# A decoder layer on Trainium2: the split chunks of the output projection moved by 192 bytes in their buffers

## The chip, the cores and the metric

The kernel runs on 1 core of one Trainium2 chip. The metric is device time in microseconds (us) of one launch; lower is better. Before the change the median of 3 runs is 1662.71 us (1659.02 to 1663.55).

## What is computed

One post-norm decoder layer on 256 tokens of width 4096, all in float32:

```python
mod = c @ w_ada[l] + b_ada[l]
shift, scale, gate = jnp.split(mod, 3, axis=-1)
u = x * (1.0 + scale[:, None]) + shift[:, None]
proj = u @ w_in[l]
...
y_rg = _rg_lru(...) * jax.nn.silu(rg_g)
y_nsa = _nsa(...) * jax.nn.silu(nsa_g)
y_hg = _hgrn2(...)
y = jnp.concatenate([y_rg, y_nsa, y_hg], axis=-1) @ w_out[l]
x = _layer_norm(ALPHA * x + (1.0 + gate[:, None]) * y, ln_g[l], ln_b[l])
```

`proj` has 11824 columns that feed three groups of heads: an RG-LRU recurrence (1024 channels), sparse attention (16 heads of 128) and an HGRN2 recurrence (8 heads of 128). `w_out` is 4096 x 4096.

## The kernel before

**Matmuls in three parts.** A float32 product is made of three matmuls in the format float32r: each operand is split into a rounded part and the rest, and hi x hi, hi x lo and lo x hi are accumulated in PSUM. Weights come in chunks of [128, up to 1024] in the order of a list of steps: `load` starts the DMA into a `raw` tile, `split` (line 1037) makes `hi` by a cast on ACT and `lo = raw - hi`, a part of the columns on DVE and the rest on POOL. When PSUM has room, DVE subtracts a second cast that ACT has put into PSUM. Four `hi` and four `lo` buffers go round.

**Order of the work.** `w_ada` is reduced on DVE to shift and scale, block by block of the 4096 input rows (10 blocks); each block's `u` is split into `uh` and `ul`, and the input projection runs over the block's chunks (`mm`, matmul on line 457). There the stationary operand is the 128 x 128 piece of the weight and the moving one is `uh` or `ul` with 256 tokens; for the groups `hg_i`, `vs` and `vw` it is the other way round, and the moving operand is the weight: 256 columns, or 304 for `vw`. In a chunk with three row blocks of `vw` the slices of 304 columns (1216 bytes) follow each other without a gap.

The output projection (`mm` with the matmul on line 969) has 128 chunks of two row blocks and 512 columns. The stationary operand is a 128 x 128 piece of `yh` or `yl`, the split output of a pair of heads; the moving one is the chunk's `hi` or `lo`, 512 columns. A chunk gives 2 token halves x 2 row blocks x 3 = 12 matmuls, so 1536 in all. `PARTS` sets the order: first the pairs 0 to 3 (RG-LRU) and 12 (HGRN2) for all eight column blocks, then 13, 14, 15, 4, 5, then the rest.

**The work between.** The heads' own work is written as fibers, Python generators that yield between pieces; `run_bg` advances them between the matmul groups of the projections when the planner's account of each engine lets it. The instructions are recorded in that order, and each engine executes its own queue in order. Lanes: RG-LRU, HGRN2, attention, and the compressed keys. A fiber of a lane starts when its inputs are done and when its slots fit in the ring (line 1189):

```python
if (all(x in done for x in need)
        and used[0] + cost + sum(max(0, r_[2] - r_[3]) for h_ in heavy for r_ in h_) <= NRING - SPARE):
```

In the HGRN2 fiber the level matmuls stand on line 708 (seven levels, each waiting for products that DVE and POOL make after the one before), the last cross term on 733, the value matmuls on 742 to 744, the sum of squares on 756, the broadcast of the norm on 769. `finish_y` then makes `yh` (ACT) and `yl` (POOL). An output chunk is recorded only once its pair is in `YT`.

**Where tiles lie.** The pool `strm` holds `raw`, `ra`, `aacc`, `hi`, `lo` and `ev`; the pool `ring` begins with a tile `shift` of `SHIFT_W` = 48 words and goes on with 62 slots of 2 KB for everything else of size [128, 512] (`u`, accumulators, the fibers' tiles, `yh`, `yl`). In the built program all `strm` buffers begin at 128 bytes past a multiple of 256, and all ring slots at 64 past one.

A helper records DVE, ACT and POOL instructions, so these show line 119 in the profile.

Of the kernel before, what the change touches and what calls it, by code (L numbers as in the profile page):

```python
# [12 lines left out]
FR = mybir.dt.float32r  # L13
# [5 lines left out]
P = 128  # L19
# [115 lines left out]
def trunk(ctx: ExitStack, tc: tile.TileContext, pack, xT, xz, w_ada, b_row, w_in, w_out, rg_w, w1, w2,  # L135
# [8 lines left out]
    strm = ctx.enter_context(tc.tile_pool(name="strm", bufs=1))  # L144
    ring = ctx.enter_context(tc.tile_pool(name="ring", bufs=1))
    psum = ctx.enter_context(tc.tile_pool(name="psum", bufs=1, space=bass.MemoryType.PSUM))
    NRING, NRAW, NSPL, NRA = 62, 4, 4, 4
    NPS = 5
    cnt = [0]
    live = [0]  # L150
# [1 line left out]
    def nm(s):  # L152
        cnt[0] += 1
        return f"{s}_{cnt[0]}"
# [13 lines left out]
    def ps_x():  # L168
        live[0] += 1
        assert live[0] <= NPS  # L170
        return psum.tile([P, 512], FT, name=nm("ps"), tag="ps", bufs=8)

    def ps_free(n=1):
        live[0] -= n
# [204 lines left out]
    def ada_end(kb, xt=None):  # L379

        n = KB[kb]
        xt = xt or load_x(kb)
        while any(r_[1] == kb for r_ in pending):
            ada_sum()
        acc = []
        for q, ps in enumerate(ada_state.pop(kb)):
            m = min(512, 2 * n * P - 512 * q)
            t_ = strm.tile([P, 512], FT, name=nm("aacc"), tag="aacc", bufs=2)
            act.copy(t_[:, :m], ps[:, :m])
            ps_free()  # L390
            acc += [t_[:, o:o + P] for o in range(0, m, P)]
        yield 1
        pp = ada_state.pop("pe") if kb == 0 else ps_x()
        for q in range(2 * n):
            nc.tensor.matmul(pp[:, q:q + 1], lhsT=acc[q], rhs=ones[:, 0:1],  # L395
                             start=kb > 0, stop=True, skip_group_check=kb == 0)
        yield 0
        md = consts.tile([P, 8], FT, name=nm("md"), tag="md", bufs=2)
        dve.tensor_add(md[:, :2 * n], pp[:, :2 * n], vec("b_mod")[:, 2 * KB0[kb]:2 * KB0[kb] + 2 * n])
        ps_free()  # L400
        dve.tensor_scalar(md[:, :n], md[:, :n], 1.0, None, op0=OP.add)
        yield from make_u(kb, xt, md[:, :n], md[:, n:])
# [25 lines left out]
    for kb in range(NKB):  # L428
        state = {}
        for items, width in chunks(kb):  # L430
            st = Step("win", off, width)
# [516 lines left out]
    for pi, part in enumerate(PARTS):  # L948
        for nb in range(NB):
            state = {}  # L950
            for ci, pr in enumerate(part):
                st = Step("wout", off_o, 1024)
# [84 lines left out]
    def split(st):  # L1037
        if not st.split:
            return
        st.hi = strm.tile([P, st.w], FR, name=nm("hi"), tag="hi", bufs=NSPL)  # L1040
        st.lo = strm.tile([P, st.w], FR, name=nm("lo"), tag="lo", bufs=NSPL)
        m = int(st.w * (1 - POOL_SHARE[st.i >= n_win0])) // 32 * 32
        if m <= 512 and live[0] < HP_PS:
            hp = ps_x()
            act.copy(st.hi, st.raw)
            act.copy(hp[:, :m].bitcast(FR), st.raw[:, :m])
            pool.tensor_sub(st.lo[:, m:], st.raw[:, m:], st.hi[:, m:])
            dve.tensor_sub(st.lo[:, :m], st.raw[:, :m], hp[:, :m])
            ps_free()
            return  # L1050
        act.copy(st.hi, st.raw)
        pool.tensor_sub(st.lo[:, m:], st.raw[:, m:], st.hi[:, m:])
        dve.tensor_sub(st.lo[:, :m], st.raw[:, :m], st.hi[:, :m])
# [5 lines left out]
    def add_at(i, f):  # L1059
        at.setdefault(i, []).append(f)  # L1060
# [8 lines left out]
    for kb in range(1, NKB):  # L1069
# [3 lines left out]
        due += [(a_ + (b_ - a_) * i / n_ch, kb, i) for i in range(n_ch)]  # L1073
        add_at(b - END_AT, lambda kb=kb: fibers.append([ada_end(kb), 1, 0, 0, 0]))
    last_part = NB * sum(map(len, PARTS[:-1]))
# [133 lines left out]
    for i in range(min(AHEAD, N)):  # L1209
        load(order[i])  # L1210
        if i < SA:
            split(order[i])
        for f in at.pop(i - LEAD, []):
            f()
# [3 lines left out]
    for i in range(N):  # L1218
        st, cur[0] = order[i], i
        if i + SA < N:  # L1220
            split(order[i + SA])
# [113 lines left out]
SPARE = 0  # L1335
MARGIN = 5
END_AT = 6


# [63 lines left out]
```

## Time and profile before

| | before |
|---|---|
| median of 3 runs, us | 1662.71 (1659.02 to 1663.55) |
| profiled execution, us | 1660.88 |
| its span, us | 1659.1 |
| mean granted TensorE clock | 0.990 |
| busy: TensorE, DVE, ACT, POOL | 96%, 80%, 59%, 58% |
| HBM read, MB | 485.12 |

The span runs from the first to the last instruction of the profiled execution; its own time is 1.8 us longer. "PE" is TensorE's matmuls, "PEld" its weight loads, which overlap them; "SPq" are DMA issues on SyncE's queue. [...] Starts in the order of time are given to 10 ns.

### The profile page before, as it was taken

To read this page: it belongs to the slowest core of one execution; us is meant where nothing else is said; L and a number is where in the kernel's file an instruction comes from. 1 tells how busy PE (TensorE), PEld (TensorE's weight loads), DVE (VectorE), ACT (ScalarE), POOL (GpSimd) and SP (SyncE) were. 2 spreads that over 40 slices of the span, in tenths; PEclk is the share of its full clock that TensorE was granted. 3 is DMA by queue.
4 is the path that set the end of the run, shared out by engine and by line. 5 is a ranking of instruction groups with operands and counts; after the bars stand their busy time and mean duration, and the time that the engine had idled before them with its cause. 6 is when DMAs were issued, how large, how long until landed. Compare 5 with 4: busy or idle time off the path is not lost.

```text
span 1659.1 us, 33161 instructions
## 1 busy us (share of the span) xinstructions
PE 1597.9 (96%) x11752; PEld 1497.6 (90%) x11752; DVE 1331.8 (80%) x2301; ACT 971.6 (59%) x1557; POOL 954.5 (58%) x765
## 2 busy tenths in 40 slices
PE   4999999999999999999999999889999999999997
PEld 4999999998999999999999998889888888878884
DVE  5668978799788788788787797899689688968875
ACT  2887666665655555555555566763565566656562
POOL 1579987776655455555455446576453445455655
PEclk9999999999999999999999998999999999999998
DMA  7998989999999899899899886767667766689983
GB/s 287 368 344 313 365 292 343 309 370 327 328 351 334 289 347 327 299 351 327 303 333 332 312 300 223 247 230 266 230 230 242 238 204 215 222 296 374 338 318 126
DMA packets 146486, 491.49 MB, mean 296 GB/s; under 512 B 16264, under 2 KB 17288, under 8 KB 146320
## 3 DMA queue, kind: packets, MB, share of 16 engines
q1 hardware_dynamic: 146320, 489.38, 82.5%
q8 instruction: 92, 1.51, 0.4%
q14 instruction: 74, 0.61, 0.1%
HBM read 485.12 MB, written 4.19 MB: 295 GB/s over the span
## 4 chain that ended last, share of the span: by engine, by line
PE 79%; DVE 11%; DMA 3%; issue 3%; ACT 3%; POOL 0%; SPq 0%; DVEq 0%; ACTq 0%
PE mm L457 50%; PE mm L969 21%; DVE ps L119 3%; DVE acc L119 2%; DVE lo L119 2%; DMA ra<-in_w_ada_dram 1%; ACT hi L119 1%; DMA raw<-in_w_in_dram 1%; PE ps L708 1%; DVE rgt L119 1%; PE ps L901 1%; PE ps L1287 1%; DVE rgy L119 1%; PE ps L792 1%; PE ps L395 1%
## 5 line engine op out<-in xcount | busy, mean ns | idle before, releaser
L119 POOL TENSOR_TENSOR lo<-raw,hi 128x576 fp32r<-128x576 f32 (+4 forms) x527 | 707.7, 1344 | 609.3 <-ACT hi L119 588.4
L119 ACT CAST hi<-raw 128x1024 fp32r<-128x1024 f32 (+3 forms) x527 | 529.1, 1004 | 487.3 <-POOL lo L119 220.4
L457 PE MATMUL mm<-uh,hi 128*128 128x256 f32 x2560 | 719.3, 281 | 15.3 <-DVE lo L119 9.2
L457 PE MATMUL mm<-uh,lo 128*128 128x256 f32 x2560 | 714.0, 279 | 1.9 <-DVE lo L119 1.4
L457 PE MATMUL mm<-ul,hi 128*128 128x256 f32 x2560 | 713.6, 279 | 0.0
L119 DVE SCALAR_TENSOR_TENSOR ps<-ra,pk,ps 128x512 f32<-128x512 f32 x744 | 520.8, 728 | 8.7 <-DMA ra<-in_w_ada_dram 2.9
L457 PEld LDWEIGHTS mm<-uh,hi 128*128 128x128 f32 x2560 | 485.3, 190 | 19.0 <-DVE lo L119 11.8
L457 PEld LDWEIGHTS mm<-uh,lo 128*128 128x128 f32 x2560 | 485.1, 189 | 2.6 <-DVE lo L119 1.9
L457 PEld LDWEIGHTS mm<-ul,hi 128*128 128x128 f32 x2560 | 485.6, 190 | 0.3 <-issue 0.2
L119 DVE TENSOR_TENSOR lo<-raw,ps 128x448 fp32r<-128x448 f32 (+4 forms) x500 | 303.2, 607 | 224.3 <-ACT ps L119 182.6
L119 ACT CAST ps<-raw 128x448 fp32r<-128x448 f32 (+4 forms) x500 | 259.5, 519 | 7.2 <-DVE acc L119 6.5
L119 DVE TENSOR_TENSOR acc<-mm,acc 128x512 f32<-128x512 f32 (+1 forms) x346 | 231.5, 670 | 0.0
L969 PE MATMUL mm<-hi,yh 128*128 128x512 f32 x512 | 210.8, 412 | 0.3 <-ACT ev L119 0.3
L969 PE MATMUL mm<-hi,yl 128*128 128x512 f32 x512 | 201.3, 393 | 0.0
L969 PE MATMUL mm<-lo,yh 128*128 128x512 f32 x512 | 200.1, 391 | 0.0
L969 PEld LDWEIGHTS mm<-hi,yh 128*128 128x128 f32 x512 | 96.4, 188 | 23.4 <-issue 5.7
L969 PEld LDWEIGHTS mm<-hi,yl 128*128 128x128 f32 x512 | 96.1, 188 | 21.6
L457 PE MATMUL mm<-hi,uh 128*128 128x256 f32 (+1 forms) x384 | 110.6, 288 | 4.9 <-ACT hi L119 3.0
L969 PEld LDWEIGHTS mm<-lo,yh 128*128 128x128 f32 x512 | 96.5, 188 | 19.1 <-issue 1.2
L457 PE MATMUL mm<-lo,uh 128*128 128x256 f32 (+1 forms) x384 | 108.9, 284 | 0.0
L457 PE MATMUL mm<-hi,ul 128*128 128x256 f32 (+1 forms) x384 | 108.9, 284 | 0.0
L119 POOL TENSOR_TENSOR acc<-ev,acc 128x512 f32<-128x512 f32 x77 | 101.2, 1315 | 2.8 <-ACT ev L119 2.5
(193 smaller groups left out, 1480.0 us busy)
## 6 DMA issues: line engine op xcount, KB each, us to landing
ra<-in_w_ada_dram SPq DMA_DIRECT2D x323, 512.0 KB, 5.8
raw<-in_w_in_dram SPq DMA_DIRECT2D x291, 512.0 KB, 5.1
raw<-in_w_out_dram SPq DMA_DIRECT2D x128, 512.0 KB, 4.6
raw<-in_w_in_dram SPq DMA_DIRECT2D x90, 384.0 KB, 5.2
ra<-in_w_ada_dram SPq DMA_DIRECT2D x64, 384.0 KB, 5.5
ra<-in_w_dram SPq DMA_DIRECT2D x16, 512.0 KB, 3.9
raw<-in_w_ada_dram SPq DMA_DIRECT2D x13, 512.0 KB, 5.6
xz<-in_xz_dram SPq DMA_DIRECT2D x16, 256.0 KB, 6.0
```

The source lines that it names most:

```text
L119: return f(*a, **k)
L395: nc.tensor.matmul(pp[:, q:q + 1], lhsT=acc[q], rhs=ones[:, 0:1], start=kb > 0, stop=True, skip_group_check=kb == 0)
L457: nc.tensor.matmul(dst, lhsT=l_, rhs=r_, start=s and n_ == 0, stop=e and n_ == 2)
L708: nc.tensor.matmul(pl[:, (2 * x + j) * 64:(2 * x + j + 1) * 64], lhsT=k[:, j, x * P:(x + 1) * P], rhs=qp[:, j, x * P:(x + 1) * P].rearrang ...
L792: nc.tensor.matmul(s1[:, b * T:(b + 1) * T], lhsT=q[:, j, P:], rhs=kk[b][:, g], start=True, stop=True)
L901: nc.tensor.matmul(o, lhsT=v0, rhs=eT[:, 0:2], start=b == 0, stop=False)
L969: nc.tensor.matmul(state[x], lhsT=a_, rhs=b_, start=ci == 0 and j == 0 and n_ == 0, stop=ci == len(part) - 1 and j == 1 and n_ == 2)
L1287: nc.tensor.matmul(pb, lhsT=rows[-1 - x], rhs=rows[i // 2][:, i % 2 * 512:i % 2 * 512 + 512], start=True, stop=True)
```

## The change

A chunk of the output projection gets tiles that are 64 words wider and uses them from word 48 on; the chunks of the input projection keep theirs from word 0. The eight buffers grow by 256 bytes each, 2 KB in all, and the ring has one slot less.

```diff
-    NRING, NRAW, NSPL, NRA = 62, 4, 4, 4
+    NRING, NRAW, NSPL, NRA = 61, 4, 4, 4
...
     def split(st):
         if not st.split:
             return
-        st.hi = strm.tile([P, st.w], FR, name=nm("hi"), tag="hi", bufs=NSPL)
-        st.lo = strm.tile([P, st.w], FR, name=nm("lo"), tag="lo", bufs=NSPL)
+
+        o = OUT_AT if st.kind == "wout" else 0
+        st.hi = strm.tile([P, st.w + o * 4 // 3], FR, name=nm("hi"), tag="hi", bufs=NSPL)[:, o:o + st.w]
+        st.lo = strm.tile([P, st.w + o * 4 // 3], FR, name=nm("lo"), tag="lo", bufs=NSPL)[:, o:o + st.w]
...
+OUT_AT = 48
```

In the built program the ring slots are still at 64 past a multiple of 256, the input projection's chunks at 128, the output projection's at 64.

With 61 slots the condition on line 1189 lets some fibers start later, so the recorded order differs from the end of the input projection on. The counts of instructions stay the same for the matmuls and DMAs.

ACT, end of the input projection, before (`hgk` and `acc_677` are tiles of the second HGRN2 fiber, `yh` is an RG-LRU fiber's output, `hi` and `ps` with `raw` are the splits of chunks, `ev` is an evacuation):

```order
L119 CAST ps_15068<-raw_14955 128x512
L119 ACT_TABLE_LOAD
L119 ACTIVATE hgk_15093<-acc_677 128x512
L119 ACTIVATE acc_677<-acc_677 128x512
L119 ACTIVATE acc_677<-acc_677,lb_5859,lb_5860 128x256
L119 ACTIVATE hgk_15093<-hgk_15093,lb_5860 128x256
L119 ACTIVATE acc_677<-acc_677,lb_5859,lb_5860 128x256
L119 ACTIVATE hgk_15093<-hgk_15093,lb_5860 128x256
L119 CAST hi_15139<-raw_15014 128x1024
L119 CAST ps_15141<-raw_15014 128x512
```

The same place now:

```order
L119 ACTIVATE hgk_15113<-acc_677 128x512
L119 ACTIVATE acc_677<-acc_677 128x512
L119 CAST yh_15128<-rgt_14757 128x512
L119 CAST hi_15131<-raw_15012 128x1024
L119 CAST ps_15133<-raw_15012 128x512
L119 ACTIVATE ev_15154<-acc_909 128x512
L119 CAST yh_15157<-rgt_14766 128x512
L119 ACTIVATE acc_677<-acc_677,lb_5859,lb_5860 128x256
L119 ACTIVATE hgk_15113<-hgk_15113,lb_5860 128x256
L119 ACTIVATE acc_677<-acc_677,lb_5859,lb_5860 128x256
L119 ACTIVATE hgk_15113<-hgk_15113,lb_5860 128x256
L119 CAST hi_15181<-raw_15046 128x1024
```

Four of the fiber's six activations have moved from ahead of this chunk's cast to behind it, and the casts of two `yh` have come up.

TensorE, the first output chunks, where the chunk of pair 12 has to wait for its fiber, before (L969 is the projection, the other lines are HGRN2 fibers):

```order
L969 MATMUL mm_16044<-hi_16017,yh_15343 128x512
L969 MATMUL mm_16044<-lo_16018,yh_15343 128x512
L969 MATMUL mm_16044<-hi_16017,yl_15344 128x512
L756 MATMUL ps_16153<-ones,hgsq_16110 128x1 x4
L742 MATMUL ps_16159<-hgA_15300,acc_705 128x128
L743 MATMUL ps_16159<-hgA_15301,acc_705 128x128
L744 MATMUL ps_16159<-hgA_15300,acc_705 128x128
L742 MATMUL ps_16159<-hgA_15300,acc_705 128x128
L743 MATMUL ps_16159<-hgA_15301,acc_705 128x128
L744 MATMUL ps_16159<-hgA_15300,acc_705 128x128
L708 MATMUL ps_16166<-hgqp_15303,hgk_15193 128x64 x4
L756 MATMUL ps_16188<-ones,hgsq_16178 128x1 x4
```

The same place now:

```order
L969 MATMUL mm_16001<-lo_15985,yh_15157 128x512
L969 MATMUL mm_16001<-hi_15984,yl_15158 128x512
L742 MATMUL ps_16113<-hgA_15271,acc_662 128x128
L743 MATMUL ps_16113<-hgA_15272,acc_662 128x128
L744 MATMUL ps_16113<-hgA_15271,acc_662 128x128
L742 MATMUL ps_16113<-hgA_15271,acc_662 128x128
L743 MATMUL ps_16113<-hgA_15272,acc_662 128x128
L744 MATMUL ps_16113<-hgA_15271,acc_662 128x128
L708 MATMUL ps_16123<-hgqp_15371,hgk_15274 128x64 x4
L733 MATMUL ps_16145<-hgqp_15234,hgk_15113 128x128 x2
L708 MATMUL ps_16149<-hgqp_15371,hgk_15274 128x64 x4
L756 MATMUL ps_16154<-ones,hgsq_16137 128x1 x4
```

The run of fiber matmuls without a projection matmul between them now begins with the first fiber's value matmuls (with `acc_662`), which stood 24 projection matmuls earlier. The last L756 of the run, the third fiber's, now follows its value matmuls without the L769 that stood between.

## Rows read from the trace of the kernel before

**Rows 1.** The page: busy time by engine, and the chain that ended last.

```profile
PE 1597.9 (96%) x11752; PEld 1497.6 (90%) x11752; DVE 1331.8 (80%) x2301; ACT 971.6 (59%) x1557; POOL 954.5 (58%) x765
...
PE 79%; DVE 11%; DMA 3%; issue 3%; ACT 3%; POOL 0%; SPq 0%; DVEq 0%; ACTq 0%
```

**Rows 2.** Stretches: length, busy time (instructions) by engine, clock, DMA share, GB/s.

```profile
1200.00:1250.00 50.00, 50.00 (x277) 42.58 (x276) 42.76 (x83) 30.69 (x60) 23.79 (x20) 1.00 0.63 216
...
1550.00:1600.00 50.00, 50.00 (x221) 41.00 (x220) 45.40 (x69) 27.79 (x38) 28.32 (x22) 1.00 0.96 350
```

**Rows 3.** A stretch, line 969 alone: length, PE (x), PEld (x), clock, DMA.

```profile
1537.95:1603.40 65.45, 65.45 (x287) 53.70 (x286) 1.00 0.94 341
```

**Rows 4.** Instructions in time, second and last of 288: start, duration in us, what.

```profile
1537.94 0.39 PE L969 MATMUL mm<-lo,yh 128*128 128x512 f32 x1
...
1603.41 0.39 PE L969 MATMUL mm<-hi,yl 128*128 128x512 f32 x1
```

**Rows 5.** Groups by shape on TensorE: busy us, mean ns of one | idle before.

```profile
L969 PE MATMUL mm<-lo,yh 128*128 128x512 f32 x512 | 200.1, 391 | 0.0
...
L901 PE MATMUL ps<-eT,acc 128*128 128x256 f32 x64 | 19.1, 379 | 0.3 <-DVE e L119 0.3
```

**Rows 6.** In time, input projection: two runs, of 12 and of 10 steps.

```profile
151.04 0.28 PE L457 MATMUL mm<-uh,hi 128*128 128x256 f32 x1
...
152.40 0.28 PE L457 MATMUL mm<-uh,hi 128*128 128x256 f32 x1
...
161.66 0.28 PE L457 MATMUL mm<-uh,hi 128*128 128x256 f32 x1
...
162.84 0.28 PE L457 MATMUL mm<-ul,hi 128*128 128x256 f32 x1
```

**Rows 7.** In time, `vw`: each row begins a triple; two chunks' halves of three.

```profile
907.43 0.30 PE L457 MATMUL mm<-hi,uh 128*128 128x304 f32 x1
...
907.85 0.30 PE L457 MATMUL mm<-hi,uh 128*128 128x304 f32 x1
...
908.27 0.30 PE L457 MATMUL mm<-hi,uh 128*128 128x304 f32 x1
...
908.68 0.30 PE L457 MATMUL mm<-hi,uh 128*128 128x304 f32 x1
...
909.09 0.30 PE L457 MATMUL mm<-hi,uh 128*128 128x304 f32 x1
...
909.51 0.30 PE L457 MATMUL mm<-hi,uh 128*128 128x304 f32 x1
...
909.92 0.30 PE L457 MATMUL mm<-hi,uh 128*128 128x304 f32 x1
```

**Rows 8.** In time, ACT and TensorE near 1090 us, with [idle before, releaser].

```profile
1086.57 0.63 ACT L119 ACTIVATE hgk<-acc 128x512 f32<-128x512 f32 x1
...
1089.70 1.04 ACT L119 CAST hi<-raw 128x1024 fp32r<-128x1024 f32 x1
...
1094.45 0.39 PE L457 MATMUL mm<-uh,hi 128*128 128x256 f32 x1 [3.03 <-DVE lo L119]
```

**Rows 9.** In time, TensorE's fiber block ahead of pair 12.

```profile
1177.63 0.39 PE L744 MATMUL ps<-hgA,acc 128*128 128x128 f32 x2
...
1184.71 0.95 PE L756 MATMUL ps<-ones,hgsq 128*128 128x1 f32 x8
...
1186.94 1.00 PE L708 MATMUL ps<-hgqp,hgk 128*128 128x64 f32 x8
1187.79 1.05 PE L756 MATMUL ps<-ones,hgsq 128*128 128x1 f32 x8
1188.94 0.71 PE L733 MATMUL ps<-hgqp,hgk 128*128 128x128 f32 x4
1190.25 1.13 PE L769 MATMUL ps<-ident,rs 128*128 128x128 f32 x8 [0.60 <-DVE rs L119]
...
1194.32 0.48 PE L969 MATMUL mm<-hi,yh 128*128 128x512 f32 x1
```

## The prediction

> **What bounds the kernel now.** I read the page first, then the stretches of time, then single matmuls. On the page TensorE is busy for 96% of the span, and the chain that ended last runs over it for 79% [rows 1]. The edit acts in the output projection, so that stage decides. In its stretches TensorE is busy for 50.00 of 50 us at the full clock, early and late, while the DMA engines rise from 0.63 to 0.96 of their time [rows 2]. So this stage is limited by the rate at which TensorE takes its matmuls, and the edit is worth what it does to that rate.
>
> The busy time of a matmul in the profile overlaps its neighbour's, so the rate has to be read from start to start. Between two gate matmuls stand 288 of the projection; the window from the second to the last holds these 287 [rows 3], which is 286 steps, 1603.41 - 1537.94 = 65.47 us, or **228.9 ns** a step [rows 4]. All 1536 matmuls of line 969 take 1536 x 0.2289 = 352 us. One nanosecond a step is 1.5 us.
>
> **The change, part by part.** The built program puts the old chunks at 128 bytes past a multiple of 256 and all ring slots, hence yh and yl, at 64 past one. The moved chunks are at 128 + 192 = 320, so at 64. The stationary yh and the moving hi or lo then begin level; before, the moving one lay 64 further on. Nothing else about these matmuls differs.
>
> *The step of the 1536 matmuls.* No matmul of this size and number format stands level in the old trace, so I bound the price by rows. Nearest is the 304-column group of the input projection (`vw`): its moving slices are 1216 bytes long, so the first of a chunk begins at 128, the second at 64, the third at 0 past a multiple of 256, all against the same stationary at 64. Its second triple is exactly the new arrangement. From triple to triple the starts are [rows 7]: first 0.42 and 0.41 us, second 0.42 and 0.42, third 0.41 and 0.41. Level triples sum to 0.84 us for six matmuls, 140.0 ns; the other four to 1.65 us for twelve, 137.5 ns. The view gives starts to 10 ns, which is 3 ns on such means. So level is dearer by about 2.5 ns here, with an error that nearly reaches zero. I take **+1.5 ns**, the low half, because one of the four other triples also shows 0.42: 1536 x 1.5 = **+2.3 us**.
>
> The two ends are farther off. *Gain:* the value product of the attention (L901) has both operands in ring slots, so it stands level already; its 256 columns in float32 are recorded at 379 ns where 512 columns here are recorded at 391 [rows 5]. If levelness is what makes the difference, a step loses 12 ns: 1536 x 12 = -18.4 us. I don't take this end because the number format and the column count differ as well. *Loss:* 256-column matmuls with one and the same placement modulo 256 step at (152.40 - 151.04) / 12 = 113.3 ns in one chunk and at (162.84 - 161.66) / 10 = 118.0 ns in another [rows 6]. So there are two rhythms 4.7 ns apart that placement alone doesn't choose; to fall into the worse one costs 1536 x 4.7 = +7.2 us. The step is steady over 286 steps, so I leave it out of the sum.
>
> [...]
>
> *The splits that write the moved chunks.* The same casts and subtractions write to other addresses; I cost this at nothing. A chunk gives TensorE 12 steps, 2.75 us; ACT's largest part of it, the 1024-column cast, takes 1.04 us [rows 8]. If a projection step fell to 217 ns the cover would still be 2.6 us.
>
> *One ring slot less.* No DMA and no compute instruction is added or dropped, on any queue. But line 1189 starts a heavy fiber only if its slots fit, and with 61 the HGRN2 fibers start later. Two places change.
>
> First, the end of the input projection. Six activations of the second HGRN2 fiber, from 1086.57 to 1089.70, 3.1 us, stand on ACT ahead of a chunk's cast, and TensorE then waits 3.03 us for that chunk's lo [rows 8]. In the new order two of them and the cast of a `yh` stand there, some 3 x 0.63 = 1.9 us, and the other four behind it. So the wait shrinks by 3.1 - 1.9 = 1.2 us: **-1.2 us**. Ends: it can go whole, -3.0 us; or the four activations and what they delay cost the next chunk as much, up to +3.0.
>
> Second, the first chunk that needs pair 12. Its four predecessors are through when TensorE goes over to fiber work alone, from 1184.71 to 1194.32 [rows 9]. In the old order the fiber's value matmuls (L742 to L744, ending after 1177.63) were 24 projection matmuls ahead of that block; in the new one they open it. Inside it two level matmuls (L708) of one fiber now have only L733 between them; from one level's matmuls to what waits for its products were 1188.94 - 1186.94 = 2.0 us, of which its own matmuls (1187.79 - 1186.94 = 0.85 us) and L733 (0.71 us) cover 1.56, so some 0.4 us are bare. And the last L756 now follows its fiber's value matmuls at once, where an L769 stood between: from the value matmuls' end to L756, with ACT's square between them, take 1187.79 - 1186.94 = 0.85 us in the old block, covered there by L708, and for the third fiber they are now bare. Together **+1.3 us**. Ends: 0, if the older levels are early enough, and +5.5 us, if all that the 24 matmuls covered (24 x 0.229) comes to light.
>
> *Sum*, against the profiled execution's 1660.9 us (span 1659.1): 1660.9 + 2.3 - 1.2 + 1.3 = 1663.3 us. That execution lies 1.8 us under the median of 1662.7, so I round up to **1664 us**, which is no change: a difference under 0.3%, 5 us, can't be told from none here.
>
> **The rivals.**
>
> *Level is faster.* The moving rows and the weights of the next matmul are read from the same memory at once; if it is the relative start that makes them meet, level may be the best case and 64 apart a bad one. For it: L901's 12 ns, and that the 512-column step (228.9) is more than twice the better 256-column one (2 x 113.3 = 226.6). Against it: the 304-column triples have the opposite sign. Time: from 3 ns (-4.6 us) to 12 ns (-18.4 us) a step; the middle, 7.5 ns, is -11.5 us, and I put it at 1650. The far end is hardly reached whole: 12 of 229 ns is 5%, and from 1550 to 1600 us the DMA engines have 4% to give [rows 2].
>
> *The later fibers are the new bound.* With the HGRN2 fibers started later, the first chunk of pair 12 waits for the whole chain behind the value matmuls, on TensorE's in-order queue, with all later chunks behind it. It decides when the chain, 1194.32 - 1177.63 = 16.7 us in the old order, of which 5.5 us lay under projection matmuls, finds nothing to hide that part. For it: the new order shows no projection matmul inside the block. Against it: in the old block TensorE stood idle for only 0.60 us before L769 [rows 9], so the fibers' own matmuls fill it. Price +5.5 us with the first place unrelieved: 1660.9 + 2.3 + 5.5 = 1668.7, slower by 0.4%.
>
> *Nothing happens.* The edit makes the starts level and the reads meet as before, because a weight load and a moving stream don't disturb each other or because they drift over all placements within one matmul. For it: the difference in the 304-column rows is about as large as their grain. Then only the order counts: 1660.9 - 1.2 + 1.3 = 1661.0. [...]
>
> **How the numbers follow.** The forecast gets 0.34, faster-by-level 0.31, later fibers 0.22, nothing 0.13. The forecast is likeliest by a little, since the only rows with the new placement in the same format have its sign. Within the forecast a tenth or so drifts over either 0.3% bound, which cancels. Faster 0.32, same 0.45, slower 0.23. The range has to reach into both other cases: down to a step 10 ns shorter, 1660.9 - 15.4 with 2 us for the order, 1643; up to the later fibers with half of the worse rhythm, 1668.7 + 3.6, 1672. Likeliest case alone: 1658 to 1668.
>
> **What would show it.** The start-to-start step between the last two gate matmuls: 230 to 231 ns if I am right, 228.9 if placement plays no role, under 226 for the faster rival. TensorE's wait for lo near 1094 should be gone or smaller, and the fiber block ahead of pair 12 should hold 1 to 2 us more idle time; over 4 us would be the slower rival. The input projection's steps and the tail after the last projection matmul must be as before; if they move, my account of the edit is wrong. A step that changes by over 3 ns in either direction makes the prediction wrong.

## The result, and the profile after

| | before | after |
|---|---|---|
| median, us | 1663.13 (4 runs) | 1677.42 (4 runs, 1676.0 to 1687.57) |
| ratio, 95% interval | | 1.0099 [1.0075, 1.0124] |
| profiled execution, us | 1660.88 | 1676.99 |
| its span, us | 1659.1 | 1675.3 |

One of the four runs before, 1788.52 us, is a slow one and left out of the ratio; the other three lie between 1659.02 and 1663.55 us. The forecast was 1664.0 us, with 1643 to 1672 as the range. The change makes the kernel 1% slower, 14.3 us by the medians and 16.1 us in the profiled executions. The sign, and one of the places, are those of the rival with the later fibers; the price is well above its 1668.7.

The page of after, the lines that answer to [rows 1]: busy time, and the chain that ended last.

```profile
PE 1602.5 (96%) x11752; PEld 1501.7 (90%) x11752; DVE 1327.3 (79%) x2301; ACT 969.8 (58%) x1555; POOL 953.6 (57%) x765
...
PE 17%; DVE 2%; issue 2%; DMA 2%; POOL 1%; ACT 1%; DVEq 0%; POOLq 0%; ACTq 0%; SPq 0%
```

The counts of matmuls are the same; ACT has two instructions fewer, since it loads its tables 16 times in place of 18. The chain covers only a small part of the span now, so it can't say where the time went; it has to be followed by other views.

Stretches of after, as in [rows 2] (length, busy time and instructions of PE, PEld, DVE, ACT, POOL, then clock, DMA share, GB/s):

```profile
1200.00:1250.00 50.00, 48.59 (x263) 41.78 (x264) 32.98 (x63) 30.11 (x56) 23.15 (x20) 0.97 0.51 174
1550.00:1600.00 50.00, 48.89 (x212) 39.46 (x212) 40.88 (x62) 26.11 (x35) 29.47 (x24) 1.00 0.89 327
```

Where TensorE was busy for 50.00 of 50 us, it now lacks 1.4 and 1.1 us, and in the first stretch the clock is at 0.97.

Groups of after by shape (busy us, mean ns of one | idle before, and what ended it), which answer to the first of [rows 5]:

```profile
L969 PE MATMUL mm<-hi,yh 128*128 128x512 f32 x512 | 209.7, 410 | 1.3 <-DVE lo L119 1.2
L969 PE MATMUL mm<-lo,yh 128*128 128x512 f32 x512 | 200.3, 391 | 2.6 <-POOL lo L119 2.6
```

The projection now waits 2.6 us for POOL's lo and 1.2 us for DVE's, where before the lo,yh group had no idle time and the hi,yh group 0.3 us. The mean duration of these matmuls is no longer (391 ns for lo,yh in both), so their time isn't where the loss is.

**Where the drift arises.** The same matmuls can be laid side by side. The last one ahead of the first difference in order (1081 us before) comes 4.3 us later than before; this is no part of the change, since the other kernels with the same instructions up to there and all input chunks at 128 lie between 2.0 us earlier and 4.7 us later. The first output matmul is 6.4 us late, the first of pair 12 (the 49th; the expectations count from 0 and call it the 48th) 13.5 us, the last 18.2 us, and the end of the span 16.2 us. So from 1081 us to pair 12 the change loses **9.2 us**, from there to the last projection matmul another **4.7**, and the tail gives 2.0 back.

### The profile page after: what moved, and what is told of

Its sections match the earlier page's. It is cut to its first block, busy times and chain, and to the rows that moved or that the text cites. A ratio compares the mean times of both kernels' runs of the same rounds, so it can differ in the third digit from the quotient of the medians.

```text
span 1675.3 us, 33160 instructions
## 1 busy us (share of the span) xinstructions
PE 1602.5 (96%) x11752; PEld 1501.7 (90%) x11752; DVE 1327.3 (79%) x2301; ACT 969.8 (58%) x1555; POOL 953.6 (57%) x765
## 5 line engine op out<-in xcount | busy, mean ns | idle before, releaser
L969 PE MATMUL mm<-hi,yh 128*128 128x512 f32 x512 | 209.7, 410 | 1.3 <-DVE lo L119 1.2
L969 PE MATMUL mm<-lo,yh 128*128 128x512 f32 x512 | 200.3, 391 | 2.6 <-POOL lo L119 2.6
L969 PE MATMUL mm<-hi,yl 128*128 128x512 f32 x512 | 200.3, 391 | 0.0
L969 PEld LDWEIGHTS mm<-hi,yh 128*128 128x128 f32 x512 | 96.3, 188 | 23.9 <-issue 4.5
L969 PEld LDWEIGHTS mm<-lo,yh 128*128 128x128 f32 x512 | 96.5, 188 | 22.6 <-POOL lo L119 4.3
L969 PEld LDWEIGHTS mm<-hi,yl 128*128 128x128 f32 x512 | 96.1, 188 | 21.0
```

The lines of the kernel that those rows point to most:

```text
L969: nc.tensor.matmul(state[x], lhsT=a_, rhs=b_, start=ci == 0 and j == 0 and n_ == 0, stop=ci == len(part) - 1 and j == 1 and n_ == 2)
```

## The experiments

Three things changed at once: the chunks' place, the number of slots in memory, and the number that the planner counts with on line 1189, which sets the order. `SPARE` is subtracted from the slots on that line, so order and memory can be changed apart.

**1 to 4: placement, slots and order apart.** The edits, each against the kernel before:

```diff
# offset_old_order: the whole change, and
-SPARE = 0
+SPARE = -1
# slot_alone
-    NRING, NRAW, NSPL, NRA = 62, 4, 4, 4
+    NRING, NRAW, NSPL, NRA = 61, 4, 4, 4
# new_order_62_slots
-SPARE = 0
+SPARE = 1
# slot_in_memory_alone: slot_alone, and
-SPARE = 0
+SPARE = -1
```

Expected of offset_old_order:

> The chunks moved by 192 bytes and 61 slots in memory, but line 1189 plans with 62, so that every engine's order is that of before. Order theory (the later fibers cost the time, the placement shortens the step from 229 to 227 ns): before - 3 us, ratio 0.998, and the fiber block ahead of pair 12 as in the old trace. Placement theory (the moved chunks cost the time, by their splits or transfers): as the changed kernel, ratio 1.010. Slot theory (61 slots in memory add waits for their reuse): 1.010 too, with the step at 227 ns.

Of slot_alone:

> 61 slots, chunks where they were: the order of the changed kernel without its placement. Order theory: the changed kernel + 3 us, 1680 us, ratio 1.011 to 1.012, step 229 ns. Placement theory: 1.000. Slot theory: 1.010.

Of new_order_62_slots:

> 62 slots in memory, chunks where they were, but line 1189 plans with 61: the new order alone. Order theory: ratio 1.010 to 1.012. Placement and slot theories: 1.000.

Of slot_in_memory_alone:

> 61 slots in memory, old order, chunks where they were. Order and placement theories: ratio 1.000. Slot theory: 1.010, with waits of TensorE or of the DMA queue for slots that the old trace doesn't have.

Measured, against a median before of 1662.9:

| kernel | order | slots | place | median, us | ratio |
|---|---|---|---|---|---|
| offset_old_order | old | 61 | new | 1662.78 | 1.0006 [0.9986, 1.0025] |
| slot_alone | new | 61 | old | 1672.68 | 1.0071 [1.0045, 1.0096] |
| new_order_62_slots | new | 62 | old | 1675.19 | 1.0081 [1.0059, 1.0103] |
| slot_in_memory_alone | old | 61 | old | 1661.71 | 1.0002 [0.9982, 1.0021] |

Both kernels with the new order are slower, neither with the old order is. The slot's 2 KB of memory cost nothing, and in the old order the new place costs nothing. So nearly all that the change costs is the order that the planner makes with one slot less. Two sizes came out otherwise than expected: offset_old_order isn't 3 us faster than before, and the order alone gives 1.0071 and 1.0081 in place of 1.010 to 1.012. The change has 1.0099, and 1.0094 in its second measurement (below). Whether the new place adds some 0.2% when it meets the new order stays open, since the intervals overlap.

**5 and 6: which part of the order.** The order differs at the end of the input projection, in the block ahead of pair 12, and, which the forecast didn't look at, again from the 204th projection matmul on: the last two gates (L414) stand behind 1164 and 1452 projection matmuls in place of 1128 and 1416. The cost of an attention fiber on line 1145 moves the late part alone:

```diff
# late_part_alone: the kernel before, and on line 1145
-                            1, 4, lambda p=p: nsa_fiber(p), 2))
+                            1, 5, lambda p=p: nsa_fiber(p), 2))
# early_part_alone: new_order_62_slots, and on line 1145
-                            1, 4, lambda p=p: nsa_fiber(p), 2))
+                            1, 3, lambda p=p: nsa_fiber(p), 2))
```

> The kernel before with the cost of an attention fiber raised from 4 to 5 slots: 62 slots, chunks at their old place, the order of before up to the 204th projection matmul, and from there the later order of the change: the last two gates (L414) after 1164 and 1452 projection matmuls in place of 1128 and 1416. Early theory (the time goes at the end of the input projection and in the fiber block ahead of pair 12): 1662.9 within 3 us, first and 48th projection matmul where they stand before, 1170.1 and 1194.3 us. Late theory (attention and gates started later starve the last third): 1668 to 1671, the 48th matmul as before, drift only after 204. If the parts add up, the late one is the 3 to 6 us that the drift in the trace of the change shows after the 480th matmul.

> The kernel before with 61 of its 62 slots given to the fibers and the cost of an attention fiber lowered from 4 to 3: the order of the change up to the 204th projection matmul (the HGRN2 fibers start later, the block ahead of pair 12 runs without projection matmuls in it), from there another order, with the last two gates after 1164 and 1452 projection matmuls as in the change. Early theory: first projection matmul 2 to 6 us later than before, the 48th 7 to 13 us later, and 1670 to 1675 in all. Late theory: 48th matmul less than 4 us later, time 1663 to 1668, since the attention starts earlier again.

Measured against 1662.0: late_part_alone 1665.13, ratio 1.0032 [1.0015, 1.0049]; early_part_alone 1679.18, ratio 1.0112 [1.0091, 1.0133]. In late_part_alone the 49th matmul stands at 1193.02 us, as early as before, and the projection waits for POOL's lo as it does in the change:

```profile
L969 PE MATMUL mm<-lo,yh 128*128 128x512 f32 x512 | 200.4, 391 | 2.2 <-POOL lo L119 2.2
```

In early_part_alone the first projection matmul is 6.8 us late and the 49th 15.3. So the early part is the larger one, and the late part costs some 0.3% by itself. The late part's time is idle time: from the 49th projection matmul to the last, TensorE's gaps add up to 0.6 us before and to 5.1 us in the change, with the clock at 1.00 in both. The two parts sum to more than the change. early_part_alone has a late order of its own that is neither the old one nor the change's, and from the 49th matmul to the last it loses another 9.7 us; its profiled execution, 1685.38 us, is also the slowest of its six.

**What the early part is made of.** The waits alone don't account for it. These are the rows of after from the end of the input projection, in order of time, with [idle before, releaser], answering to [rows 8]:

```profile
1091.59 0.39 PE L457 MATMUL mm<-uh,lo 128*128 128x256 f32 x1 [0.84 <-DVE lo L119]
...
1101.47 0.33 SPq L1032 DMA_DIRECT2D ra<-in_w_dram  x1
...
1105.03 2.77 PE L511 MATMUL ps<-kpe,ra 128*128 128x30 f32 x16 [3.51 <-DMA ra<-in_w_dram]
```

Of the wait of 3.03 us for lo only 0.84 us are left, as forecast in kind. But a wait of 3.51 us stands 13 us further on: TensorE comes to L511, and the DMA that it waits for was issued only at 1101.47. And then the clock falls. Single microseconds of after:

```profile
1104.00:1105.00 1.00, 0.00 (x0) 0.00 (x0) 0.08 (x1) 1.00 (x3) 1.00 (x2) 1.00 0.74 250
1105.00:1106.00 1.00, 0.97 (x9) 0.97 (x9) 0.00 (x0) 1.00 (x3) 1.00 (x2) 0.99 1.13 279
1106.00:1107.00 1.00, 1.00 (x7) 1.00 (x6) 0.00 (x0) 1.00 (x2) 1.00 (x1) 0.50 0.69 229
...
1112.00:1113.00 1.00, 1.00 (x8) 1.00 (x7) 0.39 (x1) 1.00 (x3) 1.00 (x2) 0.59 0.97 397
1113.00:1114.00 1.00, 1.00 (x11) 1.00 (x10) 0.90 (x2) 0.97 (x3) 1.00 (x1) 1.00 1.01 406
```

After the wait TensorE works for about 1 us at the full clock, with 9 matmuls in that microsecond, and then for six and a half at 0.50 with 6 or 7 in each; from 1113 to 1125 us it is at 1.00 again, with 10 to 12 in each. The same happens after the waits near 1142 and 1200 us, with 0.50 from 1147 to 1153 us and from 1202 to 1205 us. Three stretches of 8 us and the whole of 130 us, before:

```profile
1080.00:1210.00 130.00, 121.96 (x914) 114.78 (x914) 111.02 (x187) 69.92 (x110) 82.74 (x72) 0.99 0.69 242
1104.00:1112.00 8.00, 7.99 (x71) 7.83 (x70) 7.89 (x12) 5.51 (x10) 6.41 (x6) 1.00 0.61 213
1144.00:1152.00 8.00, 8.00 (x72) 8.00 (x71) 7.96 (x15) 2.31 (x3) 4.37 (x4) 1.00 0.89 320
1200.00:1208.00 8.00, 8.00 (x46) 6.67 (x45) 5.60 (x10) 6.95 (x15) 3.82 (x4) 1.00 0.56 163
```

and after:

```profile
1080.00:1210.00 130.00, 120.44 (x885) 115.56 (x884) 104.21 (x179) 59.43 (x92) 75.18 (x68) 0.92 0.68 235
1104.00:1112.00 8.00, 6.97 (x36) 6.97 (x37) 4.80 (x8) 5.17 (x10) 7.25 (x7) 0.62 0.71 237
1144.00:1152.00 8.00, 7.32 (x41) 6.89 (x42) 7.96 (x15) 0.67 (x2) 5.05 (x6) 0.68 0.62 208
1200.00:1208.00 8.00, 6.59 (x41) 6.41 (x42) 3.13 (x6) 3.15 (x8) 1.96 (x4) 0.79 0.04 6
```

TensorE's busy time over the 130 us hardly differs (121.96 and 120.44 us), which is why busy shares hide this; what differs is the clock, 0.99 and 0.92. In the first stretch 36 matmuls go through where 71 did; the end of the wait is 1.0 of its 8 us, and the rest is the clock. By the first rows the clock takes 130 x 0.01 = 1.3 us of work before and 130 x 0.08 = 10.4 us after, 9.1 us more, and the drift over this part is 9.2 us. In each kernel with the new order the same sum comes out within 2 us of the drift (0.01 of clock is 1.3 us, so the sum is coarse):

| kernel | clock, 1080 to 1210 us | its loss more than before, us | drift from 1081 us to the 49th, us |
|---|---|---|---|
| slot_alone | 0.93 | 7.8 | 5.9 |
| change | 0.92 | 9.1 | 9.2 |
| change_again (below) | 0.91 | 10.4 | 10.4 |
| new_order_62_slots | 0.91 | 10.4 | 10.4 |
| early_part_alone | 0.89 | 13.0 | 12.2 |

That is agreement, and not yet a cause: late products could slow the fibers whatever the clock does. And a fall doesn't always cost its sum: in the old order offset_old_order has 0.97 here, 2.6 us by the same sum, with a drift of 0.2 us. The next runs set two theories against each other. The clock theory: the time goes in the half-clock stretches behind the waits, and a clock that stays up gives it back. The data theory: the products are late at any clock.

**7 and 8: filling the waits.** change_again is the change itself; change_waits_filled keeps its order and puts matmuls of the identity, which nobody reads, right ahead of six waiting instructions (a line like the one shown stands ahead of L511, L733 and L756 too):

```diff
+    def fill(ps, n, start=True):
+        for _ in range(n):
+            nc.tensor.matmul(ps[:, 384:512], lhsT=ident, rhs=ident, start=start, stop=start, skip_group_check=True)
...
+            fill(pl, FILL.get(("level", p, L), 0))
...
+FILL = {("cmp", 1, 3): 13, ("level", 1, 4): 6, ("level", 2, 2): 3, ("level", 2, 32): 3, ("cross", 2): 6, ("square", 2): 3}
```

> The changed kernel once more, as the base for the one with filled waits: 1677 within 2 us, and in its trace again 8 to 14 us of TensorE at half clock's worth lost between 1080 and 1210 us (before: 1.7).

> The changed kernel with 34 extra 128x128 matmuls of the identity, some 0.22 us each, into unused columns of the same PSUM tiles, put on TensorE right ahead of six instructions at which its trace shows it waiting (13 ahead of one L511, 6 and 3 ahead of two early levels L708, 3 ahead of a late L708, 6 ahead of the third fiber's L733, 3 ahead of its L756). Every other instruction keeps its order. [...] Data theory (the fibers' products are late, whatever the clock): the waits behind the extra matmuls grow by what the clock gives back, and the time is 1675 to 1680; if the extra matmuls aren't hidden, up to 7.5 us more than the change.

Measured against 1660.87: change_again 1677.77, ratio 1.0094 [1.0069, 1.012]; change_waits_filled **1671.66**, ratio 1.0057 [1.0037, 1.0077]. There is more work on TensorE, and 6.1 us less time by the medians (6.3 by the means, with 2.6 to 10.4 as the 95% interval when the two kernels' runs are resampled). The stretches of change_waits_filled:

```profile
1080.00:1210.00 130.00, 124.42 (x954) 117.89 (x953) 100.94 (x175) 64.92 (x104) 77.65 (x70) 0.99 0.68 233
1104.00:1112.00 8.00, 8.00 (x71) 7.87 (x69) 5.84 (x11) 6.55 (x11) 7.28 (x6) 1.00 0.82 266
1144.00:1152.00 8.00, 8.00 (x65) 7.52 (x65) 7.93 (x17) 2.39 (x4) 3.91 (x4) 1.00 0.77 278
```

The clock is at 0.99 as before the change, and its drift from 1081 us to the 49th matmul is 5.3 us, where change_again has 10.4. Its rows in order of time (L502 are the fillers; L516, L714, L740, L764, L977 are the old L511, L708, L733, L756, L969):

```profile
1094.82 3.06 PE L502 MATMUL ps<-ident 128*128 128x128 f32 x26
...
1098.48 1.97 PE L516 MATMUL ps<-kpe,ra 128*128 128x30 f32 x16 [0.60 <-DMA ra<-in_w_dram]
...
1137.33 1.58 PE L502 MATMUL ps<-ident 128*128 128x128 f32 x12 [1.70 <-DVE hgA L119]
...
1190.56 1.58 PE L502 MATMUL ps<-ident 128*128 128x128 f32 x12
...
1195.82 0.83 PE L502 MATMUL ps<-ident 128*128 128x128 f32 x6
1196.67 1.05 PE L764 MATMUL ps<-ones,hgsq 128*128 128x1 f32 x8
1197.58 0.47 PE L977 MATMUL mm<-hi,yh 128*128 128x512 f32 x1
```

Three of these four fillers lie in what had been waits. The one at 1137.33 didn't: it had to wait 1.70 us itself, since its PSUM tile came free only when DVE was done with `hgA`. Its 6 matmuls are pure extra work, and they are a part of what the drift still holds. The clock stayed up behind this wait, where in the change, which comes to the same place after two half-clock stretches, it fell. So a wait is not followed by a fall each time. What the rest is made of can be read from the whole stretch, from the last common matmul to the 49th, in the kernel before, change_again and change_waits_filled:

```profile
1080.92:1194.33 113.41, 105.37 (x831) 100.90 (x829) 101.04 (x170) 55.78 (x84) 74.57 (x66) 0.98 0.72 255
1085.58:1209.36 123.78, 114.42 (x830) 109.55 (x829) 98.80 (x170) 55.40 (x86) 72.74 (x65) 0.90 0.69 234
1078.88:1197.59 118.71, 113.13 (x899) 108.72 (x897) 97.54 (x170) 55.39 (x86) 72.66 (x65) 0.99 0.70 244
```

Length less busy time is TensorE's idle time: 8.0, 9.4 and 5.6 us. In the last one 8.8 us of the busy time are fillers, so idle time and fillers together are 14.4 us, 5.0 more than change_again's idle time. The drift is 5.1 us smaller all the same, so the full clock gives back some 10 us. The waits behind the fillers didn't grow by that, as the data theory would have it. The 5.3 us of drift that are left are fillers longer than the waits that they fill: 14.4 us is 6.3 more than the idle time before. That the clock is most of what the early part costs is shown by this; how much a single fall costs differs from execution to execution (slot_alone, with the same order and 0.93, drifts by 5.9 us only).

**9 to 11: the chunks' place.** Two more places were tried in the old order, and one of them again with the buffers padded otherwise:

```diff
# offset_64_old_order, offset_128_old_order: offset_old_order, and
-OUT_AT = 48
+OUT_AT = 16
...
+OUT_AT = 32
# offset_128_inputs_in_place: offset_128_old_order, and
-        st.hi = strm.tile([P, st.w + o * 4 // 3], FR, name=nm("hi"), tag="hi", bufs=NSPL)[:, o:o + st.w]
-        st.lo = strm.tile([P, st.w + o * 4 // 3], FR, name=nm("lo"), tag="lo", bufs=NSPL)[:, o:o + st.w]
+        st.hi = strm.tile([P, st.w + (64 if o else 0)], FR, name=nm("hi"), tag="hi", bufs=NSPL)[:, o:o + st.w]
+        st.lo = strm.tile([P, st.w + (64 if o else 0)], FR, name=nm("lo"), tag="lo", bufs=NSPL)[:, o:o + st.w]
```

> The order of before with the output projection's chunks 64 bytes further on: the moving chunk begins at 192 past a multiple of 256, 128 past the stationary yh. If the step depends on the difference of the two starts modulo 256 (before: 64, step 229 ns; change: 0, step 227 ns): a value of its own, 226 to 230 ns. If it depends on the moving chunk's place alone (128: 229; 64: 227): again its own value. If only levelness counts: 229 ns, and 1662.9 within 2 us.

> The order of before with the chunks 128 bytes further on: the moving chunk begins at a multiple of 256, 192 past (64 ahead of) the stationary yh. If only levelness counts: 229 ns, and 1662.9 within 2 us. If the sign of the 304-column rows of the input projection holds here (those at 0 stepped 1.2 ns faster than the level ones): 226 ns, and about 1 us less than the change's placement gives.

> The order of before, output chunks 128 bytes further on (moving at a multiple of 256, yh at 64), but with buffers wider by 256 bytes, so that the input projection's chunks stay at 128 as before; in the two earlier offset runs the padding of 96 or 192 bytes moved those too. If the earlier runs' +24 us came from the input projection alone: 1664 to 1669, first projection matmul at 1170 within 3 us, and its own step 232 to 233 ns (+3.5 ns x 1536 = +5.4 us). If only levelness counts: step 229, 1662 within 2.

The first two came out at 1685.88 and 1686.77 us, ratios 1.0146 [1.013, 1.0162] and 1.0147 [1.0128, 1.0166], which none of their expectations had, and in both the first projection matmul is already 25 us late. They did more than they were meant to: the padding of o x 4 / 3 words made the buffers 96 and 192 bytes longer instead of 256, so the four `hi` buffers of the input projection began at four different places modulo 256 and no longer all at 128, and so did the four `lo`. A stretch of the input projection, first in the kernel before, then in offset_64_old_order:

```profile
500.00:550.00 50.00, 50.00 (x435) 50.00 (x435) 40.81 (x69) 27.12 (x38) 26.30 (x20) 1.00 0.91 332
```

```profile
500.00:550.00 50.00, 50.00 (x422) 50.00 (x420) 40.84 (x69) 25.62 (x37) 25.78 (x19) 1.00 0.91 324
```

At the same clock and DMA share a matmul takes 50 / 422 = 118.5 ns in place of 114.9. Over the 8832 of line 457 that is some 32 us, of which 25 arrive. offset_128_inputs_in_place has 435 matmuls in this stretch again, and its first projection matmul is 0.15 us late; it takes 1668.66 us, ratio 1.0038 [1.0022, 1.0053]. The output projection's step can now be read in a run of 118 steps behind the last gate, in all three placements with the old order. Before (moving 64 past the stationary):

```profile
1604.73 0.39 PE L969 MATMUL mm<-lo,yh 128*128 128x512 f32 x1
...
1631.74 0.40 PE L969 MATMUL mm<-hi,yl 128*128 128x512 f32 x1
```

offset_old_order (level):

```profile
1604.68 0.40 PE L969 MATMUL mm<-lo,yh 128*128 128x512 f32 x1
...
1631.46 0.39 PE L969 MATMUL mm<-hi,yl 128*128 128x512 f32 x1
```

offset_128_inputs_in_place (moving at 0, the stationary at 64):

```profile
1609.52 0.40 PE L969 MATMUL mm<-lo,yh 128*128 128x512 f32 x1
...
1637.06 0.40 PE L969 MATMUL mm<-hi,yl 128*128 128x512 f32 x1
```

The steps are 27.01 / 118 = **228.9 ns**, 26.78 / 118 = **226.9 ns** and 27.54 / 118 = **233.4 ns**. So placement does set the step, level is the best of the three, and 192 apart costs 5.2 us from the first projection matmul to the last. The traces of the other kernels agree: the median of the last 400 steps is 229 ns in all six kernels with the old place and 227 ns in all five with the level one, in either order. Over the forecast's own 286 steps offset_old_order takes 1603.36 - 1538.09 = 65.27 us, 228.2 ns, because two steps in a row there, from 1576.67 us on, last 488 and 338 ns; old_order_level_filled (below) takes 1603.57 - 1538.71 = 64.86 us, 226.8 ns. Over the whole projection offset_old_order gains 1.1 us on the kernel before.

**12: a version to beat both.** Old order, level placement, and ten fillers meant for the wait of 2.06 us ahead of an L511 at 1014.39 us, behind which the kernel before runs at half clock:

```diff
# offset_old_order, fill() as above, and
+FILL = {("cmp", 0, 0): 10}
```

> The order of before with the change's placement, and 10 of the extra matmuls (2.2 us) ahead of the first L511, where before shows a wait of 2.3 us at 1012 and then 6 us at half clock. Clock theory: clock 1.00 from 1014 to 1021, 3 us gained by 1030, of which waits for DVE's lo at 1027 to 1045 take back a part: 1658 to 1662, which would be the fastest kernel here. Data theory: 1662.8 within 1.5 us.

It took 1661.9 us, ratio 1.0007 [0.9989, 1.0026]: no gain. But the edit doesn't do what its expectation says: `("cmp", 0, 0)` is the first chunk of L511, and that one runs 40 us earlier, at 972.83 us before, without a wait. There the fillers stand:

```profile
973.26 2.39 PE L502 MATMUL ps<-ident 128*128 128x128 f32 x20
975.49 1.87 PE L516 MATMUL ps<-kpe,ra 128*128 128x30 f32 x16
```

They are 2.2 us of extra work, so the run is no test of a filled wait. The wait at 1014 us only became shorter, and the clock stayed up behind it. In order of time, before:

```profile
1014.39 3.62 PE L511 MATMUL ps<-kpe,ra 128*128 128x30 f32 x16 [2.06 <-DMA ra<-in_w_dram]
...
1028.33 0.58 PE L457 MATMUL mm<-uh,lo 128*128 128x256 f32 x1 [1.07 <-DVE lo L119]
```

and with the fillers:

```profile
1015.87 1.97 PE L516 MATMUL ps<-kpe,ra 128*128 128x30 f32 x16 [1.34 <-DMA ra<-in_w_dram]
...
1022.48 0.38 PE L457 MATMUL mm<-uh,hi 128*128 128x256 f32 x1 [1.75 <-DVE lo L119]
...
1029.71 0.58 PE L457 MATMUL mm<-uh,lo 128*128 128x256 f32 x1 [2.20 <-DVE lo L119]
```

The L511 matmuls run at the full clock (1.97 us in place of 3.62), and from 1012 to 1021.65 us the kernel goes from 2.2 us later than before to 1.6 us earlier. By 1030 it is 1.4 us late again: 3.0 of the 3.8 us have gone into waits for DVE's lo, 3.95 us in place of 1.07. Here DVE sets the pace and most of the clock's time is hidden; between 1105 and 1205 us it isn't. Why the clock fell behind 2.06 us of waiting and not behind 1.34 isn't shown. No kernel of this study beats the one before.

## Why the prediction was wrong

**"One ring slot less" is the step that failed.** It was put at -1.2 + 1.3 = +0.1 us with ends of -3.0 to +8.5, and it is nearly all of the loss: 9.8 and 12.3 us by the medians in the two kernels with the new order and the old place, of 14.3 us in the change. Three things were wrong in it.

- *Waits were priced at their own length.* Place by place the waits were not far off: the one for lo went from 3.03 to 0.84 us, and in the block ahead of pair 12 there are 0.64, 1.44 and 0.69 us of idle time where [rows 9] have 0.60, so 2.2 us more against a forecast of 1.3 (ahead of L733 0.4 us were forecast and 1.44 came, ahead of L756 0.85 and 0.69). But such a wait can be followed by 3 to 7 us at half clock, and the forecast held no term for that; from 1081 us to pair 12 it is most of the 9.2 us. The rows of after show it inside the block:

```profile
1194.15 1.10 PE L708 MATMUL ps<-hgqp,hgk 128*128 128x64 f32 x8 [0.64 <-DVE hgA L119]
...
1200.72 0.71 PE L733 MATMUL ps<-hgqp,hgk 128*128 128x128 f32 x4 [1.44 <-POOL hgk L119]
1201.27 3.35 PE L769 MATMUL ps<-ident,rs 128*128 128x128 f32 x16
...
1206.87 1.05 PE L756 MATMUL ps<-ones,hgsq 128*128 128x1 f32 x8 [0.69 <-ACT hgsq L119]
1207.79 0.48 PE L969 MATMUL mm<-hi,yh 128*128 128x512 f32 x1
```

The sixteen L769 take 3.35 us here and 1.95 us in change_waits_filled at the full clock. The trace of before had the price to show: at 1086 us, behind a wait of 0.53 us, it runs for over 3 us at 0.50. The forecast took the clock from [rows 2], where it is 1.00, and never looked at it at the end of the input projection.

- *Place 1 was looked at for one engine's queue.* The text followed ACT's. What TensorE waited for next is a load on SyncE's queue, the `ra` of L511, of which the text said nothing.

- *A third place was missed.* The order also differs from the 204th projection matmul on, with the last gates 36 matmuls later. The sentence "Two places change" was wrong; late_part_alone puts the third at 0.3%.

**The step of the 1536 matmuls had the wrong sign**: +1.5 ns taken, -2 ns measured (226.9 against 228.9 over 118 steps), and -1.1 us over the projection in place of +2.3. The 304-column rows from which it was taken are right for themselves: read to the nanosecond, the same trace has 420 and 417 ns for the level triples and 413 to 415 for the others. They don't carry over: the same relative start is a slow one there and the fast one here. The rival "level is faster" had this sign, but its lowest price was 3 ns. The rival "nothing happens" falls too, since 192 apart costs 5.2 us. It would give one step for all three placements, and the rows have 226.9, 228.9 and 233.4 ns; neither of its two reasons is shown by a run.

**What held.** The splits and the slot's memory cost nothing (1.0002 for the slot, 1.0006 with the place). The rival "the later fibers are the new bound" had the sign and one of the places; its price of 5.5 us counted the uncovered chain alone, without the clock and without the waits at 1105 and 1144 us.

## What to carry to other kernels

A buffer count that a planner reads is an edit to the order of work: undo the count and the layout apart before the layout gets the blame or the credit. Price a new wait on TensorE with what the granted clock does behind it, read in single microseconds (0.50 for 3 to 7 us here), and look whether another engine would have hidden that time anyway. When buffers are padded to move one operand, pad each by an amount that leaves the steps of the buffers' other users as they were: with 256 bytes more the input projection here kept its 435 matmuls in 50 us, with 96 more it had 422. And look in the trace whether an added instruction stands where it was meant to.

## What the runs showed of the hardware

- Behind waits of 0.5 to 3.5 us, before (at 1086 us) and in the change, TensorE ran at 0.50 of its clock for 3 to 7 us while it was busy; in change_again the 8 us from 1144 to 1152 us were at 0.58, with TensorE busy for 7.24 of them. Not every wait did this: before has 3.03 us of idle time ahead of 1094.45 [rows 8] with the clock at 1.00 afterwards. The fall shows in the matmuls, 6 or 7 in a microsecond from 1106 to 1112 us of the change, in place of 10 to 12 from 1113 us on. It needn't begin with the first matmul behind the wait: in the change the microsecond from 1105 us is at 0.99, and the next at 0.50.
- Where an operand begins modulo 256 bytes, with the other at 64, moves the step of a 512-column float32r matmul between 226.9 and 233.4 ns, and mixed places of the weights in the input projection moved 256-column steps from 114.9 to 118.5 ns. The levels don't follow one rule of relative starts over the shapes of this kernel, and what lies behind them wasn't settled.
